# Half of an output projection as seven products of block sums, the other half plainly, in turn, with the residual kept in SBUF

## The chip, the cores and the metric

One core of one Trainium2 chip. The metric is the device time of one execution of the program, in microseconds; a kernel's time is the median of its runs.

## What is computed

A block with four sequence mixers over 512 tokens of width 2048, all in float32. Each mixer gives 1024 features per token; they are gated and projected back, and the input is added:

```
h = rms_norm(x, norm_g)                       # x: 512 x 2048
p_rwkv, p_fox, p_gdn, p_diff, z = split(h @ w_in)
y = concat(rwkv7(p_rwkv), fox(p_fox), gdn(p_gdn), diff(p_diff))   # 512 x 4096
x = x + (y * silu(z)) @ w_out                 # w_out: 4096 x 2048
```

The change concerns the last line, the output projection.

## The kernel before, in words

Every large product is made of float32r matmuls: an operand v is cast to a high part (`wh`, `gh`, on ACT) and the rest is a low part (`wl`, `gl`, a subtraction on DVE); three matmuls high x high, low x high and high x low add up to one product. A matmul is 128x128 by 512 columns. Weights come from DRAM in tiles of 128x1024 float32 (512 KB, `wr`) on SP's queue; `wtile` (L323) and `wsplit` (L315 to 321) make and split them, in rings of two tiles each for `wr`, `wh` and `wl` from the pool `wp`.

The mixers come first, their matmuls in an order that a hand-written schedule sets on PE. The gated features (y * silu(z)) are numbered m = g*8 + j, with g the mixer and j one of eight slices of 128 features. Those with j below 4, called `first`, are gated beside the mixers and stored to DRAM (`gdr`, L1271), but for two `early` ones (L1273), of which the gate alone is stored and which are finished at reload. Those with j from 4 on, `second` (L1274), come after the mixers: 16 products `gemm_fm` (L326) with the z columns of `w_in`, the accumulators `acc_z`; each is gated (`gated`, L1281) and split into `gh` (L1425) and `gl` (L1426) in SBUF. Their temporaries lie in the pool `zp`; when it is closed the pool `op_b` takes its memory, so that what is written to `op_b` waits for the last use of `zp`.

The loop at L1431 to 1442 then loads the 16 stored features into `op_b` (`gr`, four buffers, POOL's queue, L1435) and splits them (ACT L1440, DVE L1441).

The output projection (L1451 to 1479) takes four column blocks nb of 512 columns. Each has four PSUM banks, one per tile of 128 tokens, and 16 weight tiles: first the eight with j from 4 on, then the eight with j below 4. A tile feeds 24 matmuls (four token tiles, two groups, three terms):

```
order = [(t, g, i) for t in range(NT) for g in range(2) for i in range(3)]
for t, g, i in order:
    a, b = parts[i]
    MM(accs[t], a[(gp + g) * NJ + q][:, t * P:(t + 1) * P], b[:, g * T:(g + 1) * T], ...)
```

That is 4 x 16 x 24 = 1536 matmuls into `acc_o`. At a block's end, for each of the four banks, a piece of x is loaded on ACT's queue (`xo`, 256 KB, six buffers, L1477), the bank is added to it (DVE, L1478) and it is stored (`out`, ACT's queue, L1479).

The order of this part is set by a scheduler from priorities (`band`): weights go ahead of evacuation (PRIO_EVAC), that ahead of feature preparation (PRIO_MIX), that ahead of the matmuls (PRIO_GEMM). Each engine runs its own list in order; an instruction that waits holds all that stand behind it on that engine. DMAs are issued by an engine too and stand in its list: SP's are weights, ACT's are the residual, the outputs and the reloads of `ydr`, POOL's are `gr`.

Of the kernel before, what the change touches and what calls it, by code (L numbers as in the profile page):

```python
# [57 lines left out]
def hybrid_kernel(ctx: ExitStack, tc: tile.TileContext, ins, out, steps=tuple(range(NJ)), ydbg=None, tail=True):  # L58
# [40 lines left out]
    wp = ctx.enter_context(tc.tile_pool(name="wp", bufs=1))  # L99
    dr = ctx.enter_context(tc.tile_pool(name="dr", bufs=1, space=DRAM))  # L100
# [196 lines left out]
    al = cp.tile([P, T], F32, name="al")  # L297
# [123 lines left out]
    lor = [cp.tile([P, T], F32R, name=f"lor{i}") for i in range(2)]  # L421
# [3 lines left out]
    gcx = cp.tile([P, 4, NT * 8], F32, name="gcx")  # L425
# [5 lines left out]
    fbias = cp.tile([P, 24], F32, name="fbias")  # L431

# [838 lines left out]
    gdr = {m: dr.tile([P, T], F32, name=f"gdr{m}") for m in first}  # L1271
# [8 lines left out]
    def gated(pool, m, acc, tags, bufs):  # L1280
# [5 lines left out]
        STT(yv, th, 0.5, yv, op0=ALU.mult, op1=ALU.mult)  # L1286
        return yv
# [130 lines left out]
    for m in second:  # L1420
# [27 lines left out]
    halves = (range(NJ // 2, NJ), range(NJ // 2))  # L1448

    sets = ("acc", "acc", "sc", "sc"), ("tr", "po", "cr", "cg")  # L1450
    for nb in range(D // T):  # L1451
        cs = slice(nb * T, (nb + 1) * T)
        accs = [bank(tag, f"acc_o{nb}_{t}", 0.0) for t, tag in enumerate(sets[nb % 2])]
        for half in range(2):
            for q in halves[half]:
                for gp in (0, 2):
                    band(PRIO_W)
                    wr = wtile()
                    nc.sync.dma_start(wr.rearrange("p (g n) -> p g n", n=T), w_out_v[:, gp:gp + 2, q, cs])
                    wh, wl = wsplit(wr)  # L1460
                    band(PRIO_GEMM)
                    first = half == 0 and q == NJ // 2 and gp == 0
                    last = half == 1 and q == NJ // 2 - 1 and gp == 2
                    parts = ((gh, wh), (gl, wh), (gh, wl))
# [42 lines left out]
```

## Time and profile before

| | |
|---|---|
| median of 3 runs | 2238.09 us (2236.98 to 2238.4) |
| profiled execution | 2235.21 us, its span 2233.4 us |
| granted TensorE clock, mean | 0.997 |
| PE busy | 2197.7 us, 98% of the span |
| PE weight loads (beside PE) | 1890.0 us, 85% |
| DVE busy | 1377.5 us, 62% |
| ACT busy | 799.5 us, 36% |
| POOL busy | 260.1 us, 12% |
| DMA | 226.34 MB, mean 101 GB/s |

Busy times are over the whole program. The sum over an engine's instructions says what it did, not what the program waited for; the chain that ended last says that. Matmuls are pipelined: the time from one to the next is shorter than the time shown for one.

### The profile page before, as it was taken

The numbers are of one execution on the slowest core, as the hardware profiler recorded it, in microseconds if no ns is written. First come the engines' busy times: TensorE is split into PE (matmuls) and PEld (weight loads), VectorE is DVE, ScalarE is ACT, GpSimd is POOL, SyncE is SP. The second block draws the span as 40 slices with busy tenths as digits, with TensorE's granted clock in tenths as the row PEclk, the third lists the DMA queues.
The fourth block names the chain that finished last, engine by engine and source line by source line (L and its number), as shares of the span: only waits on it lengthen the run. The fifth ranks groups of instructions, "written<-read, shape, count | busy, mean of one in ns | idle before, by whom it ended". The sixth has DMA issues, their size and how long they took to land.

```text
span 2233.4 us, 37352 instructions
## 1 busy us (share of the span) xinstructions
PE 2197.7 (98%) x14604; PEld 1890.0 (85%) x14604; DVE 1377.5 (62%) x3601; ACT 799.5 (36%) x1504; POOL 260.1 (12%) x538
## 2 busy tenths in 40 slices
PE   7999999999999999999999999999999999999999
PEld 6789879889978978987987897898888888888887
DVE  6478588677867858867786785885653434322222
ACT  4233443343343344334334434434322233311211
POOL 2200121103102112110210201211000000000000
PEclk9999999999999999999999999999999999999999
DMA  5433323323323332332332233244355445555443
GB/s 160 105 84 100 98 63 97 103 63 86 102 75 82 86 97 63 100 99 63 96 100 72 74 92 96 60 108 108 104 151 161 124 121 136 148 136 126 106 123 85
DMA packets 319827, 226.34 MB, mean 101 GB/s; under 512 B 17423, under 2 KB 285394, under 8 KB 319138
## 3 DMA queue, kind: packets, MB, share of 16 engines
q1 hardware_dynamic: 294114, 178.66, 30.5%
q0 software_dynamic: 11712, 23.76, 4.2%
q10 hardware_dynamic: 13824, 21.54, 2.9%
q8 instruction: 115, 1.88, 0.3%
q14 instruction: 62, 0.51, 0.1%
HBM read 203.93 MB, written 19.97 MB: 100 GB/s over the span
## 4 chain that ended last, share of the span: by engine, by line
PE 90%; DVE 3%; DMA 3%; POOL 3%; ACT 2%; issue 1%; SPq 0%; ACTq 0%; DVEq 0%; POOLq 0%
PE acc_z L75 16%; PE acc_o L75 15%; PE acc_dqk L75 8%; PE acc_vv L75 8%; PE acc_fqk L75 7%; PE acc_v L75 4%; PE acc_k L75 4%; PE acc_r L75 4%; PE acc_gv L75 3%; PE acc_gk L75 3%; PE pC L75 3%; POOL GA L842 2%; PE acc_gq L75 2%; DMA GA<-gcd 2%; PE pG L75 1%; PE pSf L75 1%
## 5 line engine op out<-in xcount | busy, mean ns | idle before, releaser
L320 DVE TENSOR_TENSOR wl<-wr,wh 128x1024 fp32r<-128x1024 f32 x318 | 388.9, 1223 | 515.6 <-ACT wh L319 513.3
L319 ACT CAST wh<-wr 128x1024 fp32r<-128x1024 f32 x318 | 333.5, 1049 | 727.3 <-PE acc_o L75 231.4
L75 PE MATMUL acc_z<-hh,wh 128*128 128x512 f32 x512 | 203.7, 398 | 0.0
L75 PE MATMUL acc_z<-hh,wl 128*128 128x512 f32 x512 | 199.7, 390 | 0.0
L75 PE MATMUL acc_z<-hl,wh 128*128 128x512 f32 x512 | 199.6, 390 | 0.0
L75 PE MATMUL acc_o<-wh,gl 128*128 128x512 f32 x512 | 183.6, 389 | 0.0
L75 PE MATMUL acc_o<-wl,gh 128*128 128x512 f32 x512 | 177.4, 389 | 0.0
L75 PE MATMUL acc_o<-wh,gh 128*128 128x512 f32 x512 | 176.3, 389 | 0.7 <-ACT wh L319 0.7
L75 PE MATMUL acc_fqk<-wh,hh 128*128 128x256 f32 x512 | 150.3, 294 | 0.0
L75 PE MATMUL acc_fqk<-wl,hh 128*128 128x256 f32 x512 | 144.6, 283 | 0.0
L75 PE MATMUL acc_fqk<-wh,hl 128*128 128x256 f32 x512 | 144.6, 282 | 0.0
L75 PE MATMUL acc_dqk<-wh,hh 128*128 128x256 f32 x512 | 138.3, 292 | 0.0
L75 PE MATMUL acc_dqk<-wh,hl 128*128 128x256 f32 x512 | 133.5, 283 | 0.0
L977 DVE TENSOR_TENSOR bP<-bX,bA 112x2 f32<-112x2 f32 (+30 forms) x248 | 122.1, 492 | 9.4 <-POOL bA L965 4.4
L75 PE MATMUL acc_vv<-wh,hh 128*128 128x256 f32 x448 | 120.3, 290 | 0.0
L75 PE MATMUL acc_vv<-wh,hl 128*128 128x256 f32 x448 | 116.8, 282 | 0.0
L75 PEld LDWEIGHTS acc_o<-wh,gh 128*128 128x128 f32 x512 | 96.1, 188 | 21.1 <-ACT wh L319 1.1
L75 PEld LDWEIGHTS acc_z<-hh,wl 128*128 128x128 f32 x512 | 96.1, 188 | 20.4
L75 PEld LDWEIGHTS acc_o<-wh,gl 128*128 128x128 f32 x512 | 96.1, 188 | 20.0
L75 PEld LDWEIGHTS acc_o<-wl,gh 128*128 128x128 f32 x512 | 96.1, 188 | 20.0
L75 PEld LDWEIGHTS acc_z<-hh,wh 128*128 128x128 f32 x512 | 96.2, 188 | 19.8 <-issue 0.3
L75 PEld LDWEIGHTS acc_z<-hl,wh 128*128 128x128 f32 x512 | 96.3, 188 | 18.7
(519 smaller groups left out, 5210.9 us busy)
## 6 DMA issues: line engine op xcount, KB each, us to landing
wr<-in_w_in SPq DMA_DIRECT2D x162, 512.0 KB
wr<-in_w_in SPq DMA_DIRECT2D x184, 256.0 KB
wr<-in_w_out SPq DMA_DIRECT2D x64, 512.0 KB
zy<-ydr ACTq DMA_DIRECT2D x30, 256.0 KB
nb<-cdr SPq DMA_DIRECT2D x8, 512.0 KB
xo<-in_x ACTq DMA_DIRECT2D x16, 256.0 KB
gr<-gdr POOLq DMA_DIRECT2D x16, 256.0 KB, 4.9
out<-xo ACTq DMA_DIRECT2D x16, 256.0 KB
```

The lines of the kernel that those rows point to most:

```text
L75: return nc.tensor.matmul(o, a, b, **kw)
L319: nc.scalar.copy(wh[:, 0:n], wr[:, 0:n])
L320: TT(wl[:, 0:n], wr[:, 0:n], wh[:, 0:n].bitcast(F32), op=ALU.subtract)
L842: nc.gpsimd.tensor_scalar(Dm[:, c, bs], Dm[:, c, bs], gcx[:, b, c * 8 + j:c * 8 + j + 1], 0.0, op0=ALU.subtract, op1=ALU.min)
L977: TT(pv_, X[:, 0:n, 0:w], A[:, 0:w, t].unsqueeze(1).to_broadcast([112, n, w]), op=ALU.mult)
```

## The change

The features' first half (j below 4) and its weights are cut into two blocks in each direction: tokens in two halves of 256, features in j 0, 1 and j 2, 3, output columns in two halves of 1024. Instead of the eight products of blocks, seven products of sums of blocks are computed (the table `products`): each has a sum or difference of two feature blocks (or one block), a sum or difference of two weight blocks (or one), and the output blocks to which its result is added or from which it is taken. The second half (j from 4 on) is multiplied plainly, as before.

- Seven products x 2 column blocks of 512 x 4 row blocks (`blocks7`) x 2 token tiles x 2 groups x 3 terms: 672 matmuls into `acc_s` (banks tr, po, cr, cg). They run in passes: products 3 and 6 together, 5, 2 and 4 together, 1 and 7 together, each over both column blocks.
- The plain half: 4 column blocks x 8 tiles x 24 = 768 matmuls into `acc_o` (banks acc, acc, sc, sc).
- The two take turns, one block of the one and one of the other, after two plain blocks at the start.
- Weights: 32 tiles for the plain half and 72 for the seven products (in a pair, a block that both products use is loaded once), 104 instead of 64; 40 of the splits take a sum made on DVE. The rings: `wr` has six tiles, `wh` and `wl` four each, two of each in `wp` and the rest in `op_b`.
- Features of the seven products: `make` loads one or two pieces of 256 KB from the stored features (`gdp`, now two groups beside each other; 48 loads on ACT's queue, ring `fr` of six), adds or subtracts them (20 times), casts and subtracts (28 of each). Products 3 and 6 are made at the start, the others during the passes ahead of them (`making`). The 16 `gr` loads on POOL's queue and their splits are gone.
- Residual: all of x lies in SBUF (16 tiles `c`, loaded at the start of the part on ACT's queue); every finished bank is added to it or taken from it (64 additions on DVE), and a tile is stored when its last contribution is in.
- The two `early` features are finished among the z products, on POOL's queue and DVE.
- Constants of the mixers move to a pool `cq` that is closed before the projection; two tiles only fill memory (`pad0`, `pad2`).

The core of the diff (left out: `cp` to `cq` for the constants, the pads, `residual`'s names of views, lines that are only moved):

```diff
+    pairs = [(q, gp) for q in range(NJ // 2) for gp in (0, 2)]
+    gdp = {p_: dr.tile([P, 2, T], F32, name=f"gdr{p_[0]}_{p_[1]}") for p_ in pairs}
...
+    products = {
+        1: (((0, 0), (1, 1), 1), ((0, 0), (1, 1), 1), ((0, 0, 1), (1, 1, 1))),
+        2: (((1, 0), (1, 1), 1), ((0, 0), None, 0), ((1, 0, 1), (1, 1, -1))),
+        3: (((0, 0), None, 0), ((0, 1), (1, 1), -1), ((0, 1, 1), (1, 1, 1))),
...
+        7: (((0, 1), (1, 1), -1), ((1, 0), (1, 1), 1), ((0, 0, 1),)),
+    }
...
-    for m in first:
-        gh[m] = op_b.tile([P, T], F32R, name=f"gh{m}")
-        gl[m] = op_b.tile([P, T], F32R, name=f"gl{m}")
-        gr = op_b.tile([P, T], F32, name=f"gr{m}", tag="gr", bufs=4)
-        nc.gpsimd.dma_start(gr, gdr[m])
...
+    def make(m, i):
...
+        for n, (t, k) in enumerate(s_ for s_ in (b, c) if s_ is not None):
+            v = op_b.tile([P, 2, H], F32, name=f"fr{m}_{i}_{n}", tag="fr", bufs=6)
+            nc.scalar.dma_start(v, gdp[q + k * HQ, gp][:, :, t * H:t * H + H])
+            vs.append(v)
+        v = vs[0]
+        if c is not None:
+            TT(v, vs[0], vs[1], op=ALU.add if sign > 0 else ALU.subtract)
+        h, l = [op_b.tile([P, 2, H], F32R, name=f"f{n}{m}_{i}", tag=f"f{n}{slots[m]}_{i}") for n in "hl"]
+        nc.scalar.copy(h, v)
+        TT(l, v, h.bitcast(F32), op=ALU.subtract)
...
+    def residual(n, cb):
+        band(PRIO_MIX)
         for t in range(NT):
-            xo = op_a.tile([P, T], F32, name=f"xo{nb}_{t}", tag="xo", bufs=6)
-            nc.scalar.dma_start(xo, x_v[:, t, cs])
-            TT(xo, accs[t], xo, op=ALU.add)
-            nc.scalar.dma_start(out_v[:, t, cs], xo)
+            c = op_b.tile([P, T], F32, name=f"c{t}_{n}_{cb}")
+            nc.scalar.dma_start(c, x_v[:, t, n * DH + cb * T:n * DH + cb * T + T])
...
+    ring = {"wr": (wp, wp, op_b, op_b, op_b, op_b), "wh": (wp, wp, op_b, op_b), "wl": (wp, wp, op_b, op_b)}
...
+    def add_to(c, at_c, acc, sign):
+        TT(c, c, acc, op=ALU.add if sign > 0 else ALU.subtract)
+        left[at_c] -= 1
+        if not left[at_c]:
+            t, n, cb = at_c
+            nc.scalar.dma_start(out_v[:, t, n * DH + cb * T:n * DH + cb * T + T], c)
...
+        passes = [(ms, cb) for ms in ((3, 6), (5,), (2, 4), (1, 7)) for cb in range(2)]
+        making = {1: (5,), 2: (2,), 3: (4,), 5: (1, 7)}
...
+                wr = {(k, n): wload(gp, q + k * HQ, n, cb) for k, n in wanted}
...
+                        TT(v, wr[b], wr[c], op=ALU.add if sign > 0 else ALU.subtract)
+                    parts[m] = halves_of(v)
+                band(PRIO_GEMM)
+                for m, t in order:
+                    fh, fl = factors[m, i]
+                    wh, wl = parts[m]
+                    for g in range(2):
+                        for s_, (a, b) in enumerate(((fh, wh), (fl, wh), (fh, wl))):
+                            MM(accs[m, t], a[:, g, t * P:(t + 1) * P], b[:, g * T:(g + 1) * T],
...
+    plain_, seven_ = plain(), seven()
+    next(plain_)
+    for i in range(len(blocks7)):
+        make(3, i)
+        make(6, i)
+        if i == 0:
+            next(plain_)
+    for n, cb in ((1, 0), (0, 0), (1, 1), (0, 1)):
+        residual(n, cb)
+    going = [seven_, plain_]
+    while going:
+        for gen in list(going):
+            try:
+                next(gen)
+            except StopIteration:
+                going.remove(gen)
```

How the engines' lists change at the start of the projection. A row gives line, operation, what is written and what is read; a number at the end of a name counts tiles. `wr` and `owr` are weight tiles as loaded, `wh` and `owh` their high parts; `fr3_1_0` is the piece 0 of product 3, row block 1 as loaded, `fh3_1` its high part; `c2_1_0` is the residual of token tile 2, column half 1, block 0. Brackets name the semaphores for which a row waits. Each DMA that SP or ACT issues takes the next of eight, DMAHW0 to DMAHW7, and waits until the DMA that had it before has landed; DMASW0 to 7 are the same for POOL's.

ACT before, at the first weight splits and the first stored features; `gr` comes by POOL's queue, so ACT has only casts here:

```order
L1277 ACTIVATE zt31_20189<-acc_z31_20132 128x512 [waits PE_49]
L1425 CAST gh31_20193<-zy31_20187 128x512 [waits DVE_49]
L319 CAST wh256_20371<-wr256_20369 128x1024 [waits DMAHW3_49,PE_49,Activation_49]
L1440 CAST gh0_20202<-gr0_20204 128x512 [waits DMAHW6_49,DVE_49,Activation_49]
L319 CAST wh257_20401<-wr257_20399 128x1024 [waits DMAHW4_49,PE_49]
L1440 CAST gh8_20211<-gr8_20213 128x512 [waits DVE_49]
L1440 CAST gh16_20220<-gr16_20222 128x512 [waits DMASW1_49]
L1440 CAST gh24_20226<-gr24_20228 128x512 [waits DMASW2_49]
```

ACT in the change, from the first load of a factor to the cast of product 3's first weights (`owh3`, whose source `owr4` holds the difference of two tiles):

```order
L1480 DMA fr3_0_0_20245<-gdr0_0_607 128x2x256 [waits DMAHW0_49,DMASW5_49,DMAHW5_49,DMASW0_49,DVE_49]
L1480 DMA fr6_0_0_20251<-gdr0_0_607 128x2x256
L1480 DMA fr6_0_1_20253<-gdr0_0_607 128x2x256
L1480 DMA fr3_1_0_20290<-gdr0_2_608 128x2x256 [waits DMAHW6_49]
L1486 CAST fh3_0_20247<-fr3_0_0_20245 128x512 [waits DMAHW7_49]
L1480 DMA fr6_1_0_20296<-gdr0_2_608 128x2x256
L1480 DMA fr6_1_1_20298<-gdr0_2_608 128x2x256 [waits DMAHW0_49]
L1497 DMA c0_1_0_20335<-in_x 128x512 [waits DMAHW1_49]
L1480 DMA fr3_2_0_20305<-gdr1_0_609 128x2x256 [waits DMAHW2_49,DVE_49]
L1497 DMA c1_1_0_20337<-in_x 128x512 [waits DMAHW3_49]
L1497 DMA c2_1_0_20339<-in_x 128x512 [waits DMAHW4_49]
L1517 CAST owh3_20378<-owr4_20373 128x1024 [waits DVE_49]
```

Eleven rows, ten of them DMAs and one a cast, stand ahead of the cast that feeds the first matmuls of the seven products; nine more residual loads and one more factor load come between this cast and the next excerpt.

ACT in the change, the end of the starting loads, and the cast for product 6 of the second row block (`owh7`):

```order
L1480 DMA fr6_2_1_20313<-gdr1_0_609 128x2x256 [waits DMAHW3_49]
L1497 DMA c0_0_1_20359<-in_x 128x512 [waits DMAHW5_49]
L1480 DMA fr3_3_0_20320<-gdr1_2_610 128x2x256 [waits DMAHW6_49,DVE_49]
L1480 DMA fr6_3_0_20326<-gdr1_2_610 128x2x256 [waits DMAHW7_49,DVE_49]
L1480 DMA fr6_3_1_20328<-gdr1_2_610 128x2x256 [waits DMAHW0_49,DVE_49]
L1497 DMA c1_0_1_20361<-in_x 128x512 [waits DMAHW1_49]
L1497 DMA c2_0_1_20363<-in_x 128x512 [waits DMAHW2_49]
L1497 DMA c3_0_1_20365<-in_x 128x512 [waits DMAHW3_49]
L1480 DMA fr5_0_0_20701<-gdr0_0_607 128x2x256 [waits DMAHW4_49,DVE_49]
L1517 CAST owh7_20453<-owr9_20445 128x1024 [waits DVE_49,PE_49]
```

All 16 residual loads and the first load for product 5 stand ahead of `owh7` now; `fr5_0_0` waits on DMAHW4.

SP in the change at the same place; `owr3` is the first tile in a buffer of `op_b`, and product 6's second block reads `owr9`:

```order
L1511 DMA owr8_20443<-in_w_out 128x2x512 [waits DMAHW4_49,DVE_49]
L1511 DMA owr3_20371<-in_w_out 128x2x512 [waits DMASW3_49,DMASW4_49,DMASW2_49,DMASW5_49,DMASW1_49,DMASW6_49,DMASW0_49,DMASW7_49,DVE_49,DMAHW0_49,PE_49,Pool_49]
L1511 DMA owr4_20373<-in_w_out 128x2x512
L1511 DMA owr5_20375<-in_w_out 128x2x512
L1511 DMA owr6_20411<-in_w_out 128x2x512 [waits DMAHW5_49]
L1511 DMA owr9_20445<-in_w_out 128x2x512 [waits DMAHW1_49,DMAHW0_49,DVE_49]
L1511 DMA owr10_20481<-in_w_out 128x2x512 [waits DMAHW4_49,DVE_49]
L1511 DMA owr11_20511<-in_w_out 128x2x512 [waits DMAHW6_49,DMAHW3_49,DVE_49]
L1511 DMA owr12_20513<-in_w_out 128x2x512 [waits DMAHW5_49,DMAHW1_49,DVE_49]
L1511 DMA owr13_20515<-in_w_out 128x2x512 [waits DMAHW4_49,DVE_49]
```

In the before all weight tiles lie in `wp`, and no row of SP waits for the end of `zp`. Now `owr3` waits for it, with all rows behind it. DMAHW4 passes from `c2_1_0` (in ACT's list) to `owr10`, then to `owr13` and to `fr5_0_0`.

## Rows read from the trace of the kernel before

**Rows 1.** The page's first lines and its chain that ended last, by engine.

```profile
span 2233.4 us, 37352 instructions
## 1 busy us (share of the span) xinstructions
PE 2197.7 (98%) x14604; PEld 1890.0 (85%) x14604; DVE 1377.5 (62%) x3601; ACT 799.5 (36%) x1504; POOL 260.1 (12%) x538
...
PE 90%; DVE 3%; DMA 3%; POOL 3%; ACT 2%; issue 1%; SPq 0%; ACTq 0%; DVEq 0%; POOLq 0%
```

**Rows 2.** The chain's last steps: start us, us, engine, tile, line, instructions.

```profile
1879.85 81.39 PE acc_o L75 x359
1964.25 5.29 DMA out<-xo
1969.95 6.96 DMA out<-xo
1978.48 250.59 PE acc_o L75 x1104
```

**Rows 3.** Groups of the out projection, 1879 to 2234 us: busy, mean ns, idle before.

```profile
L320 DVE TENSOR_TENSOR wl<-wr,wh 128x1024 fp32r<-128x1024 f32 x63 | 77.0, 1224 | 226.2 <-ACT wh L319 226.2
L319 ACT CAST wh<-wr 128x1024 fp32r<-128x1024 f32 x63 | 66.3, 1054 | 253.0 <-PE acc_o L75 231.4 <-DMA out<-xo 9.6 <-DMA wr<-in_w_out 7.6
L1478 DVE TENSOR_TENSOR xo<-acc_o,xo 128x512 f32<-128x512 f32 x16 | 10.8, 688 | 12.5 <-PE acc_o L75 12.5
L1441 DVE TENSOR_TENSOR gl<-gr,gh 128x512 fp32r<-128x512 f32 x16 | 10.6, 690 | 8.2 <-ACT gh L1440 8.0
L1440 ACT CAST gh<-gr 128x512 fp32r<-128x512 f32 x16 | 9.9, 623 | 11.7 <-DMA gr<-gdr 10.4 <-DVE gr L1439 0.9
```

**Rows 4.** Timeline of ACT, then of PE: start us, us, instruction, idle before it.

```profile
1969.56 0.35 ACTq L1477 DMA_DIRECT2D xo<-in_x  x1
1969.95 0.45 ACTq L1479 DMA_DIRECT2D out<-xo  x1
1970.43 6.83 ACTq L1477 DMA_DIRECT2D xo<-in_x  x3
1977.38 1.99 ACT L319 CAST wh<-wr 128x1024 fp32r<-128x1024 f32 x2 [9.58 <-DMA out<-xo]
...
1978.48 1.21 PE L75 MATMUL acc_o<-wh,gh 128*128 128x512 f32 x4 [0.71 <-ACT wh L319]
```

**Rows 5.** Timeline of DVE, then of POOL, at the start of the out projection.

```profile
1884.02 0.69 DVE L1426 TENSOR_TENSOR gl<-zy,gh 128x512 fp32r<-128x512 f32 x1 [0.69 <-ACT gh L1425]
...
1885.27 0.54 POOL L1435 DMA_DIRECT2D gr<-gdr  x1 [219.32 <-DVE gl L1426]
```

**Rows 6.** The tile gr: its loads and the time to landing.

```profile
L1435 POOL DMA_DIRECT2D gr<-gdr x16: 536/536/541, 1885.3 to 1911.1; - x16
...
DMA to landing us min/median/max: 2.7/4.9/6.5
```

**Rows 7.** Stretches: busy by engine, granted clock, DMA share, GB/s.

```profile
core 0: us, PE busy (x) PEld busy (x) DVE busy (x) ACT busy (x) POOL busy (x), PEclk, DMA share, GB/s
...
10.00:20.00 10.00, 8.66 (x48) 8.09 (x48) 7.71 (x16) 7.83 (x10) 6.96 (x3) 1.00 1.08 390
...
1670.00:1680.00 10.00, 10.00 (x46) 8.27 (x45) 3.01 (x4) 2.60 (x3) 0.00 (x0) 1.00 0.97 301
1885.00:1915.00 30.00, 30.00 (x134) 24.86 (x133) 17.11 (x22) 14.81 (x22) 9.64 (x18) 1.00 0.81 239
```

**Rows 8.** Stretches of 1 us around a break of PE (columns as in rows 7).

```profile
86.00:87.00 1.00, 0.42 (x5) 0.27 (x3) 0.37 (x3) 0.00 (x0) 0.00 (x0) 1.00 0.92 219
87.00:88.00 1.00, 1.00 (x6) 0.86 (x7) 0.32 (x2) 0.25 (x1) 0.00 (x0) 0.96 0.87 262
88.00:89.00 1.00, 1.00 (x4) 0.81 (x3) 0.18 (x1) 0.00 (x0) 0.00 (x0) 0.50 0.01 2
89.00:90.00 1.00, 1.00 (x3) 0.72 (x3) 0.00 (x0) 0.00 (x0) 0.00 (x0) 0.50 0.00 0
90.00:91.00 1.00, 1.00 (x5) 0.31 (x4) 0.00 (x0) 0.00 (x0) 0.00 (x0) 0.50 0.00 0
91.00:92.00 1.00, 1.00 (x10) 0.68 (x8) 0.00 (x0) 0.00 (x0) 0.00 (x0) 0.84 0.00 0
```

**Rows 9.** The tile xo: loads, additions and stores; ns min/median/max, first and last start.

```profile
L1477 ACTq DMA_DIRECT2D xo<-in_x x16: 334/448/1576, 1669.1 to 2145.8; - x16
L1478 DVE TENSOR_TENSOR xo<-acc_o,xo x16: 678/691/692, 1963.5 to 2229.1; 128x512 f32<-128x512 f32 x16
L1479 ACTq DMA_DIRECT2D out<-xo x16: 338/342/445, 1964.2 to 2229.8; - x16
```

More of the change, by code (lines that the diff above doesn't have):

```diff
@@ L419, in hybrid_kernel @@
     nlam = cp.tile([P, 1], F32, name="nlam")
-    lor = [cp.tile([P, T], F32R, name=f"lor{i}") for i in range(2)]
+    lor = [cq.tile([P, T], F32R, name=f"lor{i}") for i in range(2)]
     beta = cp.tile([P, NT, 8], F32, name="beta")
@@ L1418, in run @@
                 return e.value
-    for m in second:
+    for n, m in enumerate(second):
         acc = run(gemm_fm(Z0 + m * P, f"z{m}"))
@@ L1426, in hybrid_kernel @@
         TT(gl[m], g, gh[m].bitcast(F32), op=ALU.subtract)
+        if n < len(early):
+            band(PRIO_MIX)
+            m = early[n]
+            g, yv = [zp.tile([P, T], F32, name=f"{v}e{m}", tag=v, bufs=3) for v in ("zy", "zt")]
+            nc.gpsimd.dma_start(g, gdr[m])
+            nc.gpsimd.dma_start(yv, ydr[m])
+            STT(g, g, 0.5, yv, op0=ALU.mult, op1=ALU.mult)
+            nc.gpsimd.dma_start(gdr[m], g)
     zp_cm.__exit__(None, None, None)
@@ L1447, in hybrid_kernel @@
     out_v = out[0].rearrange("(t p) n -> p t n", p=P)
[L1448 to L1464, printed above, removed]
-                    if nb == 2:
-                        parts = ((gh, wh), (gh, wl), (gl, wh))
-                    order = [(t, g, i) for t in range(NT) for g in range(2) for i in range(3)]
-                    if nb == 1:
-                        order.sort(key=lambda o: (o[1], o[2], o[0]))
-                    for t, g, i in order:
-                        a, b = parts[i]
-                        MM(accs[t], a[(gp + g) * NJ + q][:, t * P:(t + 1) * P], b[:, g * T:(g + 1) * T],
-                           start=(first and g == 0 and i == 0), stop=(last and g == 1 and i == 2))
-        for t in range(NT):
-            band(PRIO_EVAC)
-            xo = op_a.tile([P, T], F32, name=f"xo{nb}_{t}", tag="xo", bufs=6)
-            nc.scalar.dma_start(xo, x_v[:, t, cs])
-            TT(xo, accs[t], xo, op=ALU.add)
-            nc.scalar.dma_start(out_v[:, t, cs], xo)
@@ new lines, in hybrid_kernel @@
+    blocks7 = [(q, gp) for q in range(HQ) for gp in (0, 2)]
+    slots = {3: 0, 6: 1, 5: 0, 2: 1, 4: 0, 1: 1, 7: 0}
+    factors = {}
+    def make(m, i):
+        band(PRIO_MIX)
+        q, gp = blocks7[i]
+        b, c, sign = products[m][0]
+        vs = []
+        for n, (t, k) in enumerate(s_ for s_ in (b, c) if s_ is not None):
[8 more added lines that the diff above has]
+        TT(l, v, h.bitcast(F32), op=ALU.subtract)
+        factors[m, i] = h, l
@@ new lines, in hybrid_kernel, with wnext, wload, halves_of @@
+    turn = dict.fromkeys(ring, 0)
+    def wnext(tag, dtype):
+        pool = ring[tag][turn[tag] % len(ring[tag])]
+        turn[tag] += 1
+        return pool.tile([P, WN], dtype, name=f"o{tag}{turn[tag]}", tag=tag, bufs=ring[tag].count(pool))
+    def wload(gp, q, n, cb):
+        wr = wnext("wr", F32)
+        nc.sync.dma_start(wr.rearrange("p (g n) -> p g n", n=T),
+                          w_out_v[:, gp:gp + 2, q, n * DH + cb * T:n * DH + cb * T + T])
+        return wr
+    def halves_of(v):
+        wh, wl = wnext("wh", F32R), wnext("wl", F32R)
+        nc.scalar.copy(wh, v)
+        TT(wl, v, wh.bitcast(F32), op=ALU.subtract)
+        return wh, wl
```

94 lines of the change are left out of this document (73 added, 21 removed), and 3 rows, old and new, of the table products.

## The prediction

> **What bounds the kernel now.** The page comes first: PE is busy for 98% of the span and takes 90% of the chain that ended last [rows 1]. So a change counts by the TensorE time it takes away and by the idle time it puts in. The chain's last rows are the out projection: matmuls into acc_o from 1879.85 us on, a short hand-over to ACT's transfers at 1964 to 1977, then matmuls to the end [rows 2]. The two rows of matmuls give the pace: 81.39 / 359 and 250.59 / 1104 are both 0.227 us. The 389 ns of one record in the group rows is pipelined and is no price. The stage has 1536 matmuls; 1536 x 0.227 is 348.7 us, so from 1879.5 to 2228.9 PE hardly waits. The other engines have room: of some 350 us DVE spends 77.0 + 10.8 + 10.6, ACT 66.3 + 9.9 [rows 3].
>
> **What goes.** The first features' half of the stage is 768 matmuls. Seven products, 2 column blocks, 4 row blocks, 2 token tiles, 2 groups and 3 terms are 672, each of the same form (128x128 by 512 columns). 96 x 0.227 = **21.8 us** less. The before has one stall of its own, 0.71 us of PE, when ACT stood 9.58 us behind the transfers of the residual [rows 4]; with the residual kept in SBUF that reload is gone: **0.7 us** less. Together 22.5.
>
> **What comes and lies beside PE.** DVE goes from 98 to 242 instructions in the stage: 88 splits and 40 sums of two weight tiles (128 x 1.22 = 157 us), 28 + 20 for the factors, 64 additions into the residual and 2 early gates (114 x 0.69 = 79 us) [rows 3]. 236 us in some 327 of PE: not the bound on average. In the densest passes, (3, 6), a pair of blocks (24 + 24 matmuls, 10.9 us) needs 5 x 1.22 + 3 x 0.69 = 8.2 us of DVE; it fits with 2.7 to spare. ACT: 88 x 1.05 + 28 x 0.62 + 80 transfers to issue at 0.45 [rows 3, 9] = 146 us. The four added weight halves (wh and wl rings of 4 instead of 2) let ACT and DVE run three splits ahead of PE, so once this runs I take most delays as hidden. The end is as before: one addition, one transfer out after the last matmul (2229.1 to 2233.4 [rows 1, 9]). The early gates move into the z part, where DVE is less than half busy; they cost nothing, and if they did, one wait of DVE's, some 3 us, would show on PE there.
>
> **What comes and lies on the path: the start.** In the before the new pool's memory comes free only when the last z tile is split: DVE gl at 1884.02, 0.69 long, and POOL's first load follows [rows 5]. The same wait stands on the change's first factor load and on SP's first weight tile from that pool. So nothing of the seven products' operands moves before 1885.1, 5.6 us after the last z matmul, and the two plain blocks put ahead cover 48 x 0.227 = 10.9 us, to 1890.4. In the before nothing here was urgent: the stored features were needed 32 tiles of weights later than now.
>
> The order shows what then stands in line. Every transfer of SP and ACT takes one of eight semaphores and waits for the one that held it before; ACT's casts stand in the same queue behind such waits. The cast of product 3's first weights stands behind two residual loads that wait for the sixth transfer; the cast of product 6's second block (owh7) stands behind 16 residual loads and fr5_0_0, which waits on DMAHW4: c2_1_0, owr10, owr13, fr5_0_0 go through that semaphore one after the other. So owh7 waits until owr13 has landed, and by then 9 tiles of 524 kB and 19 of the 21 loads of 262 kB issued around them have moved: 4.7 + 5.0 = 9.7 MB. PE without a wait would be at owh7's matmuls after 48 + 24 + 24 + 12 = 108 matmuls, at 1879.5 + 24.5 = 1904.0.
>
> When can owh7 be ready? 1885.1, plus 1.8 us that a transfer takes beside its bytes (2.7 us is the fastest landing of 262 kB [rows 6], less 0.9 at 300 GB/s), plus 9.7 MB at the rate B, plus 1.5 for an issue and the cast: 1888.4 + 9.7 / B. PE's loss is that less 1904.0. The earlier gaps (the first weights: 2.4 MB, ready near 1895.7 where PE is free at 1890.4) are part of it, not added. No row shows the SP and ACT queues both full with these tiles, so B is bounded from both sides: 390 GB/s, at the kernel's start with many loads queued, is the most over 10 us; 301 in 1670 to 1680, six residual loads of ACT beside SP's weights; 239 in 1885 to 1915, this very place, where loads waited for buffers and less was asked for [rows 7]. Losses: 9.3, 16.6 and 25.0 us. Eight transfers in flight resemble the first two; I take 340, between them: **12.9 us**.
>
> By the Trainium skill (DMA: Bandwidth & Descriptors, Specifications and Issuing engines are not separate DMA queues) loads from two issuing engines share the same 16 DMA engines, with a ceiling of 435 GB/s; at that ceiling the loss would be 22.3 - 15.6 = 6.7 us, an estimate from that page. The trace agrees that it isn't reached over 10 us: 390 at most [rows 7].
>
> **The clock.** After a break near 86 us the granted clock stood at 0.50, which is 1.2 GHz, from 88 to 91 and came back to 2.4 GHz [rows 8]: 0.5 x 3 and a little at the edges, 1.7 us lost. The 0.71 us stall at 1978 had no such fall. The start's gaps are several microseconds; falls that come before the last gap only shorten that gap, since the loads set its end, so I count one: **1.7 us**. Between 0, if the fall hits what waits anyway, and 5.1 for three.
>
> By the Trainium skill (TensorE: Matmul & The Clock Gate, HAM oscillation) each wait for data in a burst of matmuls can bring the half clock anew; with three such falls outside the gaps the sum would be 3.4 us worse.
>
> **Later passes.** ACT keeps issuing factor loads and output transfers between casts. The before shows what one such hold costs: 9.58 us on ACT, 0.71 on PE with a lookahead of one split [rows 4]. With three I take one such loss in all, **0.7 us**; bounds 0 and 5.6, one at each of eight pass ends.
>
> **The sum.** 22.5 - 12.9 - 1.7 - 0.7 = 7.2 us less. The profiled execution takes 2235.2 (span 2233.4 and 1.8 around it), 2.9 below the median of 2238.1; the median moves alike: **2231**.
>
> **Rivals.**
> 1. *The start is cheap.* B is 390 or more, or owr13 lands ahead of the residuals. For it: the 390 of the kernel's start [rows 7]. Against: ACT's and SP's queues wait for each other, so the eight are not always in flight. With 9.3 us and no clock fall: 22.5 - 9.3 = 13.2, 2225; with the first two gaps alone (4.3 and 1.9 at 390) 16.3, 2222.
> 2. *The start eats the gain: slower.* One mechanism: the first loads at 239 GB/s, as measured at this place. 25.0 + 1.7 + 0.7 = 27.4 against 22.5: 2243. It decides the sign below 9.7 / (22.5 - 2.4 + 15.6) = 272 GB/s. For it: 1 kB runs of the factor loads, and the 239 itself. Against: that window had fewer transfers queued.
> 3. *ACT's queue holds PE at every pass.* Eight losses of 0.7 instead of one: 22.5 - 12.9 - 1.7 - 5.6 = 2.3, 2236, no change that can be told. For it: 80 issues among the casts. Against: three splits of lookahead, 8 to 11 us.
> 4. *The gain is whole.* No stall, 2216. Against it the fixed 5.6 us and the 2.4 MB before product 3: even at 390 GB/s PE waits 4.3 us.
>
> That the change does less than it says is excluded for PE: 96 rows fewer stand in its order.
>
> **Chances.** About 0.2% (4.5 us) is what a measurement of this kernel can tell from no change: 2233.6 and 2242.6 are the bounds. Forecast, 2226 to 2236: 0.45. Rival 1, 2220 to 2226: 0.22. Rival 2, 2240 to 2250: 0.17. Rival 3, 2233 to 2240: 0.12. Rival 4: 0.04. Of the forecast about 0.34 lies below 2233.6. Faster 0.34 + 0.22 + 0.04 = 0.60; slower 0.15 (most of rival 2); no change 0.25. The range takes in rivals 1 and 3 and the nearer half of 2: **2220 to 2245**.
>
> **What would show it.** Right: acc_o and acc_s matmuls together 1440; PE idle 5 to 7 us near 1890 before the first acc_s, released by ACT owh, and once more before owh7's matmuls near 1911 to 1918; DMA above 300 GB/s from 1887 to 1915; the granted clock at 0.5 for some 3 us after; then matmuls at 0.227 us with idle time below 2 us to the end. Wrong: idle time in the passes after 1930, released by DVE sums or by weight loads, makes DVE or the lanes the bound; no idle time at the start makes 2216; a pace above 0.227 for the new matmuls breaks the first term.

## The result and the profile after

The changed kernel takes **2252.85 us** (2250.35 to 2255.48), the one before 2238.2 beside it: 1.0068 times as long, 95% interval 1.0056 to 1.0081. It is slower by 14.7 us, where 7.2 less were forecast, and lies above the range (2220 to 2245). The two profiled executions lie 18.7 us apart (2253.9 and 2235.2); the stages below are theirs.

The page of the profiled execution (2253.9 us) first; its lines answer to [rows 1]:

```profile
span 2251.8 us, 37580 instructions
...
PE 2185.8 (97%) x14508; PEld 1875.4 (83%) x14508; DVE 1499.5 (67%) x3745; ACT 829.5 (37%) x1540; POOL 254.3 (11%) x526
...
PE 81%; DMA 7%; DVE 6%; POOL 3%; ACT 2%; issue 2%; ACTq 0%; SPq 0%; DVEq 0%; POOLq 0%
```

PE does less (2185.8 against 2197.7 us), and the end is 18.4 us later. Its share of the chain fell from 90% to 81%; what came in is DMA (7%, 3% before) and DVE (6%, 3%). So the new time is mostly waiting time. TensorE's timeline gives each wait in brackets, with what ended it (the two long ones, and three of the seven that follow):

```profile
1903.63 0.80 PE L75 MATMUL acc_s<-owh,fh 128*128 128x512 f32 x1 [10.98 <-ACT owh L1517]
...
1926.02 0.79 PE L75 MATMUL acc_s<-owh,fh 128*128 128x512 f32 x1 [6.29 <-ACT owh L1517]
...
2071.17 0.47 PE L75 MATMUL acc_s<-owh,fh 128*128 128x512 f32 x1 [2.84 <-DVE c L1522]
...
2185.73 0.50 PE L75 MATMUL acc_s<-owl,fh 128*128 128x512 f32 x1 [1.62 <-DVE owl L1518]
...
2211.56 0.47 PE L75 MATMUL acc_s<-owh,fh 128*128 128x512 f32 x1 [2.99 <-DVE c L1522]
```

The last z matmul starts at 1881.4, the last of all at 2247.0: 365.6 us for the stage, 349.2 before (1879.5 to 2228.7). 1440 matmuls at 0.227 are 326.9; the nine waits add up to 27.6, of which 17.3 are the two at the start; 11.1 are left. Nearly all of that is matmuls at half the clock, as these stretches show (columns as in [rows 7]):

```profile
1885.00:1924.00 39.00, 23.75 (x94) 18.83 (x92) 15.06 (x17) 7.50 (x10) 0.00 (x0) 0.80 0.97 295
1904.00:1908.00 4.00, 4.00 (x10) 3.11 (x10) 2.90 (x3) 2.97 (x4) 0.00 (x0) 0.50 0.99 325
1926.00:1932.00 6.00, 5.98 (x14) 4.72 (x15) 5.43 (x6) 3.00 (x4) 0.00 (x0) 0.50 0.98 298
2072.00:2074.00 2.00, 2.00 (x7) 1.57 (x6) 1.96 (x3) 0.00 (x0) 0.00 (x0) 0.55 0.85 182
2213.00:2215.00 2.00, 2.00 (x6) 1.57 (x5) 2.00 (x4) 1.04 (x1) 0.00 (x0) 0.50 0.88 192
```

After each wait of 2.8 us or more the granted clock is 0.50 (1.2 GHz; 0.55 where the stretch takes in the fall): 10 matmuls in 4 us instead of 18. The first line has the rate of the start, 295 GB/s, with 1.7 us ahead of the first load in it; the view of the DMA queues from 1886.6 to 1924.3, in which the loads ran, has 303:

```profile
DMA packets 7531, 11.41 MB, mean 303 GB/s; under 512 B 540, under 2 KB 3404, under 8 KB 7529
```

That the last z matmul is 1.9 us later can't be put down to the change: the same matmul starts between 1879.3 and 1883.5 in the profiled executions of the experiments, whose work up to there is the same, and from 1500 us to it PE waits nowhere, before or after. So the early gates in the z part cost PE nothing, as forecast.

DVE is about as busy as the prediction had it (227 us, 236 forecast; three groups of it from 1881.5 on, to be read against [rows 3]; the last column is the idle time before them):

```profile
L1518 DVE TENSOR_TENSOR owl<-owr,owh 128x1024 fp32r<-128x1024 f32 x87 | 104.6, 1221 | 42.7 <-ACT owh L1517 42.5
...
L1571 DVE TENSOR_TENSOR owr<-owr,owr 128x1024 f32<-128x1024 f32 x40 | 48.9, 1223 | 75.4 <-DMA owr<-in_w_out 75.2
...
L1522 DVE TENSOR_TENSOR c<-c,acc_s 128x512 f32<-128x512 f32 x48 | 30.2, 682 | 4.3 <-PE acc_s L75 4.1
```

Half of DVE's 150 idle us it waits for weight tiles (75.2), standing at a sum. Two places show what that costs PE. ACT's timeline at the start (ACTq are its DMA issues; several of one kind in a row are one line):

```profile
1899.30 3.19 ACTq L1497 DMA_DIRECT2D c<-in_x  x2
1902.53 1.04 ACT L1517 CAST owh<-owr 128x1024 fp32r<-128x1024 f32 x1 [6.89 <-DMA fr<-gdr]
...
1917.88 3.19 ACTq L1480 DMA_DIRECT2D fr<-gdr  x3
1921.11 2.70 ACTq L1497 DMA_DIRECT2D c<-in_x  x3
1924.30 0.53 ACTq L1480 DMA_DIRECT2D fr<-gdr  x1
1924.93 1.99 ACT L1517 CAST owh<-owr 128x1024 fp32r<-128x1024 f32 x2 [11.11 <-DMA fr<-gdr]
```

The residual's issues (`c`) take 3.19 us for two and 2.70 for three, because each waits for a semaphore; behind the first of these stands the cast of product 3's first weights, behind the second and `fr5_0_0` (1924.30) the cast `owh7`. That is the queue that the prediction read from the order. The second gap is all of that list: DVE had made the last sum for the first two row blocks at 1915.8 (the row below), before PE came to `owh7`'s matmuls at 1919.7, and the cast began at 1924.93. SP stood too, between 1884 and 1926, and for the same residual loads, whose semaphores its weights take next (us in all, times, longest):

```profile
1914.54 1.22 DVE L1571 TENSOR_TENSOR owr<-owr,owr 128x1024 f32<-128x1024 f32 x1
...
SPq L1511 <- DMA c<-in_x: 27.0, 4, 15.6
```

DVE late in the kernel, in two rounds of products 1 and 7 (a round is one block of the seven products and one plain block; `owr` is a sum of two weight tiles, `owl` a low half, `c` an addition into the residual):

```profile
2184.45 3.49 DVE L1518 TENSOR_TENSOR owl<-owr,owh 128x1024 fp32r<-128x1024 f32 x3
2193.40 1.23 DVE L1571 TENSOR_TENSOR owr<-owr,owr 128x1024 f32<-128x1024 f32 x1 [5.45 <-DMA owr<-in_w_out]
2195.43 1.23 DVE L1571 TENSOR_TENSOR owr<-owr,owr 128x1024 f32<-128x1024 f32 x1 [0.81 <-DMA owr<-in_w_out]
2196.58 3.49 DVE L1518 TENSOR_TENSOR owl<-owr,owh 128x1024 fp32r<-128x1024 f32 x3
2205.96 1.22 DVE L1571 TENSOR_TENSOR owr<-owr,owr 128x1024 f32<-128x1024 f32 x1 [5.90 <-DMA owr<-in_w_out]
2207.86 1.23 DVE L1571 TENSOR_TENSOR owr<-owr,owr 128x1024 f32<-128x1024 f32 x1 [0.68 <-DMA owr<-in_w_out]
2209.00 1.22 DVE L1518 TENSOR_TENSOR owl<-owr,owh 128x1024 fp32r<-128x1024 f32 x1
2210.14 2.48 DVE L1522 TENSOR_TENSOR c<-c,acc_s 128x512 f32<-128x512 f32 x4
```

The three splits start at 2184.45 and again at 2196.58: a round takes 12.1 us, though PE needs 10.9 for it. In between DVE waits 5.45 us for a weight tile. The chain that ended last names the circle (24 matmuls, at their pace, then the circle):

```profile
2167.34 5.44 PE acc_o L75 x24
2172.78 5.44 PE acc_s L75 x24
...
2184.45 3.50 DVE owl L1518 x3
...
2187.97 7.37 DMA owr<-in_w_out
...
2196.58 3.50 DVE owl L1518 x3
...
2200.09 7.67 DMA owr<-in_w_out
```

The splits end at 2187.97, then a tile takes 7.4 us to land, then come its sum and the splits. The six buffers hold a round and a half of four tiles, so the next tiles are asked for when the splits free some, and no earlier. At a pass's end the additions (2210.14) that free PE's banks stand behind those sums, and PE waits 2.99 us for them.

The wait of 2.84 us at 2071 is not of that circle. There the additions stand behind a sum of two factor pieces, which waits for its load:

```profile
2068.00 0.69 DVE L1484 TENSOR_TENSOR fr<-fr,fr 128x512 f32<-128x512 f32 x1 [5.84 <-DMA fr<-gdr]
...
2069.75 2.48 DVE L1522 TENSOR_TENSOR c<-c,acc_s 128x512 f32<-128x512 f32 x4
```

### The profile page after: what moved, and what is told of

It reads as the page before. It is cut to its first block, busy times and chain, and to the rows that moved or that the text cites. A ratio compares the mean times of both kernels' runs of the same rounds, so it can differ in the third digit from the quotient of the medians.

```text
span 2251.8 us, 37580 instructions
## 1 busy us (share of the span) xinstructions
PE 2185.8 (97%) x14508; PEld 1875.4 (83%) x14508; DVE 1499.5 (67%) x3745; ACT 829.5 (37%) x1540; POOL 254.3 (11%) x526
## 4 chain that ended last, share of the span: by engine, by line
PE 81%; DMA 7%; DVE 6%; POOL 3%; ACT 2%; issue 2%; ACTq 0%; SPq 0%; DVEq 0%; POOLq 0%
PE acc_z L75 16%; PE acc_dqk L75 8%; PE acc_vv L75 8%; PE acc_fqk L75 7%; PE acc_k L75 4%; PE acc_v L75 4%; PE acc_r L75 4%; PE acc_s L75 4%; PE acc_o L75 3%; PE acc_gv L75 3%; PE acc_gk L75 3%; DMA owr<-in_w_out 3%; PE pC L75 3%; POOL GA L847 2%; DMA fr<-gdr 2%; PE acc_gq L75 2%
## 5 line engine op out<-in xcount | busy, mean ns | idle before, releaser
L323 DVE TENSOR_TENSOR wl<-wr,wh 128x1024 fp32r<-128x1024 f32 x254 | 310.7, 1224 | 285.6 <-ACT wh L322 283.3
L322 ACT CAST wh<-wr 128x1024 fp32r<-128x1024 f32 x254 | 266.2, 1048 | 472.3 <-PE acc_z L75 158.1
L1517 ACT CAST owh<-owr 128x1024 fp32r<-128x1024 f32 x88 | 91.4, 1052 | 242.1 <-PE acc_s L75 54.5
L1518 DVE TENSOR_TENSOR owl<-owr,owh 128x1024 fp32r<-128x1024 f32 x88 | 105.8, 1221 | 44.2 <-ACT owh L1517 44.0
L75 PE MATMUL acc_s<-owh,fh 128*128 128x512 f32 x224 | 90.9, 407 | 24.1 <-ACT owh L1517 17.3
L75 PE MATMUL acc_dqk<-wl,hh 128*128 128x256 f32 x512 | 103.0, 283 | 0.0
L75 PE MATMUL acc_o<-owh,gh 128*128 128x512 f32 x256 | 99.8, 390 | 0.0
L75 PE MATMUL acc_o<-owh,gl 128*128 128x512 f32 x256 | 99.8, 390 | 0.0
```

Source lines behind the costliest of these rows:

```text
L75: return nc.tensor.matmul(o, a, b, **kw)
L322: nc.scalar.copy(wh[:, 0:n], wr[:, 0:n])
L323: TT(wl[:, 0:n], wr[:, 0:n], wh[:, 0:n].bitcast(F32), op=ALU.subtract)
L1517: nc.scalar.copy(wh, v)
L1518: TT(wl, v, wh.bitcast(F32), op=ALU.subtract)
```

## The experiments

Each run's stage is worked out as above: from the last z matmul's start to the last matmul's, less 326.9 us of matmuls, less PE's waits; the rest is nearly all matmuls at half the clock. The time is a median; the kernel before took 2238.0 to 2238.8 beside them. The last four columns are of the one profiled execution, whose own time stands ahead of them: where it lies far from the median (seven buffers, late and seven), so do they.

| kernel | time, us | ratio to before (95%) | profiled, us | stage | waits before 1940 | waits later | rest |
|---|---|---|---|---|---|---|---|
| before | 2238.2 | | 2235.21 | 349.2 | 0 | 0.7 | |
| the change | 2252.85 | 1.0068 (1.0056 to 1.0081) | 2253.93 | 365.6 | 17.3 | 10.3 | 11.1 |
| late residual | 2244.95 | 1.0026 (1.0015 to 1.0037) | 2245.21 | 355.7 | 8.7 | 9.9 | 10.2 |
| residual on POOL | 2251.4 | 1.0058 (1.0043 to 1.0073) | 2251.95 | 365.3 | 13.0 | 12.4 | 13.0 |
| six plain blocks | 2249.46 | 1.0051 (1.0036 to 1.0066) | 2248.63 | 360.1 | 9.3 | 14.2 | 9.7 |
| seven buffers | 2245.1 | 1.0030 (1.0019 to 1.0040) | 2241.57 | 355.7 | 14.0 | 6.2 | 8.6 |
| late and seven | 2233.52 | 0.9978 (0.9968 to 0.9988) | 2230.22 | 343.2 | 8.1 | 5.2 | 3.0 |
| and factors on POOL | 2233.84 | 0.9980 (0.9970 to 0.9990) | 2236.17 | 346.2 | 8.2 | 5.1 | 6.0 |
| and six plain | 2233.04 | 0.9981 (0.9971 to 0.9991) | 2232.93 | 344.9 | 3.0 | 8.8 | 6.2 |
| and four plain | 2229.57 | 0.9962 (0.9947 to 0.9976) | 2231.16 | 341.4 | 3.5 | 6.4 | 4.6 |
| four plain, blocks at pass ends | 2229.24 | 0.9959 (0.9946 to 0.9971) | 2229.24 | 341.2 | 3.4 | 4.8 | 6.1 |
| that, halves on POOL | 2233.88 | 0.9979 (0.9971 to 0.9988) | 2236.3 | 347.5 | 7.9 | 6.0 | 6.7 |
| four plain, halves on POOL | 2235.8 | 0.9989 (0.9980 to 0.9998) | 2235.41 | 346.9 | 6.5 | 6.5 | 7.0 |

### The start: bytes or ACT's queue

Late residual:

```diff
-            nc.scalar.dma_start(c, x_v[:, t, n * DH + cb * T:n * DH + cb * T + T])
+            nc.gpsimd.tensor_copy(c[:, 0:1], latest[0].bitcast(F32)[:, 0:1])
+            nc.gpsimd.dma_start(c, x_v[:, t, n * DH + cb * T:n * DH + cb * T + T])
...
+    due = {2: (1, 0), 3: (0, 0), 5: (1, 1), 9: (0, 1)}
```

> The 16 residual loads leave ACT's queue for POOL's, and each set of four waits for the low weight half of a later row block (one value of it is copied into the tile ahead of the load), so 4.2 MB leave the first 35 us. Start gaps of the changed kernel: 11.0 and 6.3 us. If bytes set them (theory B): 4.2 MB / 0.34 = 12 us of the 17.3 go, and one clock fall of 2 to 3 us: 2238 to 2241. If the place of ACT's casts behind the residual loads sets them (theory Q): product 3's first cast moves from 1902.5 to 1897.6, where its operand is made, 5 us, and the second gap falls to some 2: 8 to 9 us and one fall go: 2241 to 2244. If it is the late release of the pool's memory that counts: 2250 or more.

Residual on POOL, without the copy and at the old place:

```diff
-            nc.scalar.dma_start(c, x_v[:, t, n * DH + cb * T:n * DH + cb * T + T])
+            nc.gpsimd.dma_start(c, x_v[:, t, n * DH + cb * T:n * DH + cb * T + T])
```

> The same 16 residual loads on POOL's queue, without the added wait: all are issued when the pool's memory comes free, so the bytes of the start stay, and only ACT's queue and the eight semaphores are rid of them. Theory Q: as the run before, 2241 to 2245. Theory B: the bytes come even earlier, the weights and factors behind them no sooner: 2252 to 2257, the first gap 11 us or longer.

Measured: 2244.95, a little above both theories, and 2251.4, just below the bytes theory and far above the queue's. TensorE's waits at the start, first of the late residual, then of the residual on POOL:

```profile
1900.63 0.79 PE L75 MATMUL acc_s<-owh,fh 128*128 128x512 f32 x1 [6.32 <-ACT owh L1519]
...
1902.98 0.79 PE L75 MATMUL acc_s<-owl,fh 128*128 128x512 f32 x1 [0.27 <-DVE owl L1520]
```

```profile
1898.78 0.80 PE L75 MATMUL acc_s<-owh,fh 128*128 128x512 f32 x1 [7.30 <-ACT owh L1517]
...
1905.75 0.73 PE L75 MATMUL acc_s<-owh,fh 128*128 128x512 f32 x2 [1.72 <-ACT fh L1486]
1907.47 0.80 PE L75 MATMUL acc_o<-owh,gh 128*128 128x512 f32 x1 [0.98 <-ACT owh L1517]
...
1923.05 0.50 PE L75 MATMUL acc_s<-owh,fh 128*128 128x512 f32 x1 [3.00 <-ACT owh L1517]
```

With ACT's queue free, but the same bytes, the first cast starts at 1897.7 instead of 1902.5 and the waits fall from 17.3 to 13.0 us, half of what the queue theory had. The time hardly follows (1.5 us, within the spread of the change's own runs): PE now runs in pieces between four waits, at half the clock over much of 1898 to 1910 (0.64 granted on average), 1.9 us more of the rest, and two new waits have come at 1971 and 1985 (1.39 and 1.05 us). Without the bytes as well, the waits at the start are 8.7, and 7.9 us of time go. So both theories hold a part: in the waits at the start equal ones (4.3 us each), in the time the bytes the larger one. With the list free the sums themselves come late, as the last cast before PE's wait of 3.00 us shows:

```profile
1921.95 2.00 ACT L1517 CAST owh<-owr 128x1024 fp32r<-128x1024 f32 x2 [2.50 <-DVE owr L1571]
```

The forecast of 2241 to 2245 for the queue alone was wrong.

### The start: cover

```diff
+            pool = wp
...
+            return pool.tile([P, WN], dtype, name=f"p{tag}{nahead[0]}", tag=tag, bufs=2)
...
-            next(plain_)
+            for _ in range(5):
+                next(plain_)
...
+            if gen is plain_ and rounds[0] in (9, 11, 13, 15):
+                continue
```

> Six plain blocks instead of two ahead of the first product (in the two weight buffers that are free early), four fewer beside product 5. 21.8 us more of cover. Theory B: both start gaps (17.3 us) and two clock falls (5.3 us) go, the later gaps stay: 2230 to 2234. Theory Q: the casts of the plain blocks' weights now stand behind the residual and factor loads in ACT's list, and PE waits for them too: at least one wait of several us released by a high weight half in 1890 to 1920, 2236 to 2246.

Measured 2249.46, outside both. PE waits inside the plain blocks themselves:

```profile
1904.23 0.50 PE L75 MATMUL acc_s<-owh,fh 128*128 128x512 f32 x1 [3.13 <-ACT owh L1523]
...
1920.94 0.80 PE L75 MATMUL acc_o<-pwh,gh 128*128 128x512 f32 x1 [5.95 <-ACT pwh L1523]
```

The 5.95 us end with ACT's cast of a plain block's weights (`pwh`), as the queue theory said. The waits at the start fell by 8.0 us, not by 17.3, and the time by 3.4: cover is worth little while its own casts stand behind the loads it is to hide. The later waits grew too, by 3.9 us.

### The later rounds: one buffer more

```diff
-    ring = {"wr": (wp, wp, op_b, op_b, op_b, op_b), ...
+    ring = {"wr": (wp, wp, op_b, op_b, op_b, op_b, op_b), ...
```

> One weight buffer more (seven instead of six), nothing else. Theory L (later gaps come of a loop: three splits free buffers, the next tiles take 7.4 us to load, then two sums, then the splits; 12.1 to 12.4 us a round against 10.9 of PE's): the six gaps from 2160 on (7.4 us) and the clock fall after 2211 (1.7) shrink by 5 to 9 us: 2244 to 2248. Rival: the order of DVE's list, additions behind sums that wait for loads, sets them, and a buffer more changes less than 2 us: 2251 to 2253. The start stays.

Measured 2245.1, 7.8 us less, within the loop theory's range. DVE's waits from 2100 to 2250 us (us in all, times, longest), first of the change, then with seven buffers:

```profile
DVE owr L1571 <- DMA owr<-in_w_out: 50.7, 16, 6.1
```

```profile
DVE owr L1571 <- DMA owr<-in_w_out: 32.5, 11, 6.9
```

The wait for weights falls from 50.7 to 32.5 us, PE's later waits from 10.3 to 6.2. That the start would stay was wrong: 3.3 us went there too (SP waits 10.4 us for residual loads there, 27.0 in the change), and slow matmuls fell by 2.5. So the time fell into the range with the start's help: the later waits gave 4.1 us of the 9.9 by which the profiled stage is shorter. What is left of the later waits sits where DVE's list has additions or splits behind a sum whose tile is late.

### Together, and further

Late residual and seven buffers, the two diffs above:

> The late residual loads on POOL's queue and the seventh weight buffer together. The two alone gave 7.9 and 7.8 us less than the changed kernel (2252.85). If start and later rounds are separate losses, they add: 2252.9 - 15.7 = 2237, 2234 to 2240. If both shortened the same gaps (the buffer also lets a weight tile more load at the start: the second gap was 3.0 us instead of 6.3 there): 2240 to 2244.

Measured 2233.52, 0.5 below the better case's range: 19.3 us less than the change, and 3.6 more than the sum of the two, which the spread does not make sure (seven buffers alone took 2241.57 to 2248.5). At the start they overlap: the waits fall by 9.2 us, by 8.6 and 3.3 alone. In the profiled execution, the shortest of its eight, the rest is 3.0 us instead of 11.1, since one wait at the start (8.05 us) is left, and none later is followed by the half clock. This version is faster than the kernel before.

The factor loads on POOL's queue as well:

```diff
-            nc.scalar.dma_start(v, gdp[q + k * HQ, gp][:, :, t * H:t * H + H])
+            nc.gpsimd.dma_start(v, gdp[q + k * HQ, gp][:, :, t * H:t * H + H])
```

> As the run before, and the 48 factor loads too leave ACT's queue for POOL's: ACT has only casts and the 16 output transfers, and the eight semaphores serve weights and outputs alone. If casts behind waiting factor loads still cost (theory Q: the first gap, 6.3 us with the residual gone, falls to the 4 us in which the first operands come): 2 to 4 us below the run before. If the bytes and the release of the pool's memory set what is left: within 1.5 us of it. If POOL's issues (0.54 us each) and its order delay the factors: up to 5 us above it.

Measured 2233.84: no difference. The start's waits are 4.65 and 3.51 us instead of one of 8.05. What is left there is not ACT's queue.

That with six, and with four plain blocks at the start (the residual's first two sets a round or so earlier, since they are needed sooner):

```diff
-            next(plain_)
+            for _ in range(3):
+                next(plain_)
...
+            if gen is plain_ and rounds[0] in (9, 13):
+                continue
```

> As the run before, with six plain blocks at the start and four fewer beside product 5. Nothing of ACT's queue can hold the plain blocks now but the factors' casts. If the start's gaps are a matter of cover: no PE wait above 1 us and no clock fall before 1930, some 8 to 11 us less than the run before, 2225 to 2230, clearly faster than the kernel before the change (2238). If the cover is lost later, where four rounds of product 5 stand without a plain block (12 matmuls, 2.7 us, for a weight tile each): new waits near 2010 to 2050, and less than 4 us gained.

> As the run before with four plain blocks at the start and two fewer beside product 5: 10.9 us more of cover than the change has instead of 21.8. If 6 to 9 us of start gaps are left without it, nearly the same as with six: within 2 us of that run. If the six cost something at product 5, this one is the faster.

Measured 2233.04 and 2229.57: no gain with six, 4.3 us with four. Cover works at the start now: 3 to 3.5 us of waits are left of 8.2. Six plain blocks cost later (8.8 us of later waits, 6.4 with four), less at the end of product 5, where I had expected it (1.40 us at 2051, 0.55 with four), than at the ends of passes from 2140 on. The 3.52 us that remain with four blocks have this behind them, PE's wait and then DVE:

```profile
1899.92 0.50 PE L75 MATMUL acc_o<-pwl,gh 128*128 128x512 f32 x1 [3.52 <-DVE pwl L1526]
...
1887.88 0.69 DVE L1450 TENSOR_TENSOR gl<-zy,gh 128x512 fp32r<-128x512 f32 x1 [0.69 <-ACT gh L1449]
1897.50 1.23 DVE L1580 TENSOR_TENSOR owr<-owr,owr 128x1024 f32<-128x1024 f32 x1 [8.93 <-DMA owr<-in_w_out]
1898.65 1.22 DVE L1526 TENSOR_TENSOR pwl<-pwr,pwh 128x1024 fp32r<-128x1024 f32 x1
```

The sum of the first two tiles from the new memory waits 8.93 us for its load, and the low half of a plain block (`pwl`) stands behind it; its high half had been done at 1893.2.

Two plain blocks more moved to the ends of passes, rounds 24 and 28:

```diff
-            if gen is plain_ and rounds[0] in (9, 13):
+            if gen is plain_ and rounds[0] in (9, 11, 13, 15):
                 continue
...
+                if gen is plain_ and rounds[0] in (24, 28):
+                    next(gen)
```

> The run with four plain blocks at the start (2229.6 us), and two more plain blocks moved: from beside product 5 to the ends of the passes at which PE waited for additions (2.3 us and a clock fall of 1.9 after the second pass of products 2 and 4; 1.2 us between the passes of 1 and 7). If the missing cover between two passes is what those waits are (the additions, 6 to 8 x 0.69 us behind two sums, against 5.4 us of one plain block): 4 to 6 us less, 2224 to 2226. If the additions are held by sums that wait for weights, and cover only moves the wait: within 1.5 us of 2229.6.

Measured 2229.24, the same as 2229.57. Of the two waits at which it aimed, that of 2.32 us is gone and in place of that of 1.18 one of 1.13 us ends with a low weight half at 2195; and one of 2.48 us with a half clock (0.51 from 2044 to 2046) has come at 2043, at the end of product 5, from where the blocks were taken: the wait was moved, as the second theory has it.

The low halves of the third and fourth plain block on POOL, in the last version and in the one before it:

```diff
+        if 0 < nahead[0] <= 12 and not late_sub.append(0) and len(late_sub) in (3, 4):
+            nc.gpsimd.tensor_tensor(out=wl, in0=v, in1=wh.bitcast(F32), op=ALU.subtract)
+        else:
             TT(wl, v, wh.bitcast(F32), op=ALU.subtract)
```

> As the run before, and the low weight halves of the third and fourth plain block are made on POOL (2.5 us each instead of 1.2 on DVE). If DVE's order holds them (a sum of two weight tiles stands ahead and waits 8.9 us for its load; PE waits 3.5 us and loses 1.7 to the clock): 3 to 5 us less than the run before. If POOL's own order (a factor load that waits for a buffer stands ahead of the fourth) holds them instead: less than 1.5 us.

> Four plain blocks at the start as in the 2229.6 us run, with the low halves of the third and fourth on POOL and nothing else. The same two theories as for the run before: 2225 to 2227 if DVE's order is what makes the last wait of the start, 2228.5 to 2231 if it is not.

Measured 2233.88 and 2235.8, 4.6 and 6.2 us slower, outside both theories. On POOL the fourth half started at 1900.80 and 1898.93, behind a factor load that waits for a buffer, so POOL's own order did hold it; and PE's list had come out otherwise, with matmuls of product 3 ahead of plain ones, so that PE met the late weights with less cover (5.48 and 2.41, 3.75 and 2.77 us). Whether the half behind the sum sets the last 3.5 us is thus not shown.

## Why the prediction was wrong

The stage was to be 7.2 us shorter and is 16.4 longer, 23.6 us off (21.9 by the medians): 7.2 at the start, 6.6 by the clock, 9.6 in the later passes. By its terms:

- **The matmuls removed**: 21.8 us. Right: the rows of 24 matmuls in the chain take 5.44 us, 0.227 each, in `acc_s` as in `acc_o`.
- **The start**: 12.9 us forecast. By the same measure, the second gap's end against a PE that never waits, 20.1 are measured: 1926.0 less 1905.9 (1881.4 + 24.5); that is the two waits, 17.3, and the matmuls at half the clock between them. The mechanism was right: two gaps where they were named, ended by the two casts that were named, with the residual's bytes and their place in ACT's queue behind them. The size was off, in two terms. The rate: I took 340 GB/s between bounds, and it was 303; 9.7 MB at 303 take 3.5 us more. The nearest row was that of 1670 to 1680 (301 [rows 7]), which I had put at 16.6 us. The bytes, the larger term: "19 of the 21 loads of 262 kB" goes by the turn of the semaphores, but the order lists 29 such loads in front of `owh7`, and 11.4 MB had moved when it came, not 9.7: 5.6 us at 303. The two make 9.1 us where 7.2 have to be explained; so the parts beside the bytes had been put some 2 us too high. By the Trainium skill (DMA: Bandwidth & Descriptors, Issuing engines are not separate DMA queues) the two queues share the same engines; the trace agrees as far as it goes: with both full it moved 303 GB/s, where SP's weights beside six residual loads had moved 301 in the old kernel.
- **The clock**: 1.7 us forecast for one fall behind the start, 8.3 measured (11.1 less the 2.8 that lie in the start). That the first fall only shortens the second gap held. The step that failed is "so I count one": after the second gap the matmuls lose 3.0 us, after the waits of 2.84 and 2.99 us 1.7 each, and the five short waits a few tenths each. PE did not wait again for 140 us after the second gap and for 85 after the third, so nothing came there that a fall could have shortened. The rule of the Trainium skill that the text weighed (TensorE: Matmul & The Clock Gate, HAM oscillation: each wait for data in a burst of matmuls can bring the half clock anew) was the better guide; the trace agrees with it in four waits of the nine; after those of 1.62, 0.94 and 0.97 us the granted clock stayed at 1.00.
- **Later passes**: 0.7 us forecast, 10.3 measured. The largest step that failed: that the added weight halves "let ACT and DVE run three splits ahead of PE, so once this runs I take most delays as hidden", and "236 us in some 327 of PE: not the bound on average". Both looked at busy time and at the halves' rings. What came instead is what the prediction had named as a sign of being wrong, idle time after 1930 released by DVE. In the last passes the bound is the circle through the six buffers of loaded tiles: free, load (7.4 us), sum, split, 12.1 us for a round of 10.9. No term of mine had it. One buffer more took 7.8 us off the time, and 4.1 us off the later waits. The circle is not all of them: the wait of 2.84 us came behind a factor's load, and 6.2 us are left with seven buffers; no run changed DVE's order there, nor was it tested why a tile takes 7.4 us to land.

The rival that it was, "the start eats the gain", had its place and sign right and a rate of 239 GB/s, which did not come; 272 was its limit, and the measured 20.1 us alone would have left 2.4 of the 22.5. With the clock and the later rounds the change was slower. The range ended at 2245 because it took in only the nearer half of that rival; all three upper bounds (25.0, 5.1 and 5.6 us) make 2251, still below what was measured. Those of the clock and the later passes were priced from the old kernel's one hold and one fall, though 48 matmuls of the new rounds need four tiles where the old ones needed two.

## What to carry to other kernels

A weight that is summed, split and multiplied passes through buffers whose turn-round (free, load, sum, split) must be set against the matmuls of a round; busy shares and a lookahead counted in the last ring alone do not show it. Put transfers that are needed late behind something that is ready late, on a queue that no urgent work stands in, before adding cover. And price each wait of several microseconds on TensorE twice, the wait and the matmuls at half the clock behind it: removing one wait can be worth little if it leaves several short ones.

The two best versions here, 2229.57 and 2229.24 us, are 0.4% faster than the kernel before and can't be told from each other; some 8 to 10 us of waits are still in them.

## What was not expected of the hardware

- The half clock came after waits of 1.97 us (factors on POOL, at 2062: 0.68 granted over the next 3.5 us) and 2.32 us (four plain blocks, at 2147: 0.50), and not after one of 2.22 us (late and seven, at 2058: 1.00) nor after 2.40 (six plain blocks, at 2155: 1.00); the length of the wait alone does not tell it.
- With the residual on POOL's queue beside SP's and ACT's loads, the stretch 1898 to 1910 ran at 385 GB/s, and the mean of 1885 to 1924 was 322 instead of 295: with a third queue asked the rate was higher, but over half of the bytes of 1898 to 1910 were the residual's, for which nothing waits. Whether the queue or the smaller share of 1 KB pieces raised the rate was not tested.
- With four plain blocks at the start, the first two tiles of 524 kB from the new memory, which one sum needs, were usable some 9 us after the memory came free (DVE's wait of 8.93 us, above), with more weight tiles and six factor loads asked for at once; a single 262 kB load there took 2.7 to 6.5 us [rows 6].
